# Gate biases beside their products, and earlier operand loads for the recurrence, in a two-layer diffusion step

## The chip, the cores and the metric

The kernel runs on 1 core of a Trainium2 chip. The metric is the device time of one execution in microseconds (us), lower is better. Times of a kernel are given as the median of several runs; a profile comes from one more execution, whose own time is given beside its span.

## The reference, cut to what matters

One inference step of a two-layer hybrid backbone (model width 1024) on 256 context tokens and 1024 latent tokens. Layer 0 combines grouped-query attention (8 query heads, 2 key heads of 64) with a bidirectional RWKV-7 recurrence (8 heads of 64); layer 1 is gated linear attention (GLA). Each layer is modulated: a vector m of 3072 numbers gives shift, scale and gate.

```
m = silu(cond) @ mod_w[i] + mod_b[i]
shift, scale, gate = split(m, 3)
h = rms_norm(x, norm_g[i]) * (1 + scale) + shift
out = mixer_i(h)                  # i = 0: attention + RWKV-7, i = 1: GLA
x = x + gate * out

# attention: 128-query blocks, keys and values of the cache (512) and the latent tokens (1024)
p = softmax(q @ k.T * 64 ** -0.5);  o_a = (p @ v) * silu(ga)

# RWKV-7, per head, forward and backward over the tokens
sa = s @ (-kk_t)
s  = s * w_t + outer(sa, kk_t * a_t) + outer(v_t, k_t)
y_t = s @ r_t
```

## The kernel before, in words

The program is recorded by a scheduler of its own (`Sched`), which holds a planned start for each engine, queue and tile. The kernel's parts are written as *streams* of *tasks* (generators). `drive` looks at the next dozen instructions of each running task, plans when each could start, and records the one with the lowest planned start; where two engines could do an operation it picks one. So the instruction order on every engine comes out of planned costs, and one edit can move a great many rows. All instructions are recorded through one line (L357), which is why all rows carry that line; the tile names tell what they are. `get(tag)` takes a tile of a tag's set of buffers, `put` gives it back, `sch.until(cond)` holds a task until a flag is set.

Phases in the order of time: norms and modulation; the projections of layer 0, the last of which are those of the gates (`gated`, tiles `gt`, two buffers); then the *mixers* of layer 0, about 510 to 1340 us; output projection; layer 1. This case turns on the passage from the gate projections into the mixers. There these streams run beside each other:

- `room_attn` and `room_rwkv` make room: they close the pools of the phase that ends, open new ones, and write the constants of the new phase. `room_attn` allocates KA, KB (keys of the two key heads; KA the high, KB the low part and a row of ones), VO (values) and the query tiles QA, QB, and fills the unused rows of KB on POOL (GpSimd), 4 memsets. `room_rwkv` waits until the eight gate projections are over (it takes over their SBUF), then loads the masks (gmask, zmask, m1) and makes id16, m116, hm, id2, the fills of UV, LL and Z, and the ring of states, and at its end sets flag `rwkv`.
- `rwkv_seg`: 40 tasks (4 head pairs x 5 segments of 256 tokens x 2 directions), 4 at a time. Each loads AR, BK and Vs (3 buffers each), scales with `pair` by the decays, multiplies AR by BK on PE (TensorE), inverts a triangular matrix in five rounds (tiles TT, Tm, LT, Z), builds GR, UV, U, GH, and carries the state along (tile `ring`).
- `maxima` (one task per unit of 512 or 256 queries): scores KA x QA, a maximum over each row on DVE (VectorE; `mx`), and at the end of 12 such products one transpose (`ident,mx`) whose result goes into QB as the row's offset.
- `attend`: for each block of 128 keys the pair QA x KA + QB x KB, exp on ACT (ScalarE), and the product with VO. It waits for flag `keys`.
- `keys` loads KB and VO once `attn` is set.
- `mods`: 16 chunks of 256 columns of the modulation, for layer 0's gate and for layer 1. Of each, `mod_cols` loads 1 MB of weights (`mw`, 1 buffer) and multiplies them by sT (16 matmuls); the 8 gate chunks also load a bias row. Products lie in tile m4 (1 buffer), and the bias in a `gt` tile.

The bias tile is the one that the gate projections use, two buffers in all:

```
b = yield from get(row, False)        # row = "gt"
D.dma_start(out=b[0:2, 0:n], in_=I["mod_b"][...].to_broadcast([2, n]))
```

All loads named here go through SP's queue, in SP's order; each load waits there until an earlier one of at most 8 has landed.

## Time and profile before

| | |
|---|---|
| median of 3 runs | 2095.14 us (2094.4 to 2097.18) |
| the profiled execution | 2095.28 us, its span 2093.5 us |
| busy share of the span: PE, DVE, ACT, POOL | 95%, 69%, 48%, 14% |
| mean granted clock of PE | 0.984 of full |
| share of the chain that ended last: PE, DVE, issue, ACT, DMA | 52%, 11%, 4%, 3%, 1% |
| PE busy from 560 to 1240 us | 664.32 of 680 us |
| PE busy from 510 to 540 us | 5.31, 6.37 and 7.61 in stretches of 10 us |

How to read it: the median of runs and the profiled execution differ by 0.14 us, so sums below are made against 2095.28. PE is busy nearly all the time, but not evenly; the profile cuts the span in 40 slices, and the digit of PE is below 9 in four of them: the first, the tenth (about 471 to 523 us, with the passage into the mixers), the 26th (about 1309 to 1361 us, the output projection) and the last. A slice is 52 us, so gaps of a few us are seen only in the timeline.

### The profile page before, as it was taken

What the parts mean: (1) busy time and instruction counts of PE and PEld (TensorE: products, weight loads), DVE (VectorE), ACT (ScalarE), POOL (GpSimd) and SP (SyncE); (2) the same over time, 40 slices, a digit from 0 to 9 for tenths busy, and PEclk for the clock granted to TensorE, in tenths of its full rate; (3) what the DMA queues carried; (4) which work ended last, traced back from release to release, by engine and by line L of the source; (5) the groups of instructions that cost most, each with busy time, mean ns of one, the idle gap of its engine ahead of it and who ended that gap; (6) DMA issues with size and microseconds to landing.
All of it is one profiled execution on the core that took longest, in us unless ns stands there. A gap on an engine that the chain in (4) does not pass through costs nothing.

```text
span 2093.5 us, 38539 instructions
## 1 busy us (share of the span) xinstructions
PE 1997.0 (95%) x14876; PEld 1557.7 (74%) x14876; DVE 1452.4 (69%) x2879; ACT 1007.6 (48%) x2184; POOL 289.9 (14%) x383
## 2 busy tenths in 40 slices
PE   6999999998999999999999999799999999999998
PEld 4878687886667777777776766578778888888886
DVE  4677866777887888778888987453575656564455
ACT  4454744553556655665656563333445454542111
POOL 2010200013221112121110020010121111110011
PEclk9999999999999999999999999899999999999999
DMA  8224342527513241323223224342102011115653
GB/s 297 71 101 159 138 164 81 179 91 238 170 54 103 81 143 59 97 74 111 78 68 88 67 70 143 95 146 73 50 14 64 28 50 29 49 31 165 192 170 112
DMA packets 215143, 219.56 MB, mean 105 GB/s; under 512 B 16480, under 2 KB 161232, under 8 KB 214960
## 3 DMA queue, kind: packets, MB, share of 16 engines
q1 hardware_dynamic: 214960, 217.10, 33.0%
q8 instruction: 117, 1.92, 0.4%
q14 instruction: 66, 0.54, 0.1%
HBM read 149.63 MB, written 67.39 MB: 104 GB/s over the span
## 4 chain that ended last, share of the span: by engine, by line
PE 52%; DVE 11%; issue 4%; ACT 3%; DMA 1%; POOL 0%; SPq 0%; POOLq 0%; DVEq 0%; ACTq 0%
PE a L357 26%; PE pj L357 26%; DVE QQ L357 2%; DVE LL L357 1%; DVE mx L357 1%; ACT QQ L357 1%; DVE TT L357 1%; DVE dec L357 1%; DVE gt L357 1%; DVE Z L357 1%; DVE y L357 1%; DVE GR L357 0%; DVE KX L357 0%; DVE GH L357 0%; DVE Ad L357 0%
## 5 line engine op out<-in xcount | busy, mean ns | idle before, releaser
L357 PE MATMUL pj<-hhi,whi 128*128 128x512 f32 (+1 forms) x672 | 241.1, 361 | 2.6 <-DVE whi L357 1.4
L357 PE MATMUL pj<-hhi,wlo 128*128 128x512 f32 (+1 forms) x672 | 240.4, 360 | 1.6 <-DVE wlo L357 1.6
L357 PE MATMUL pj<-hlo,whi 128*128 128x512 f32 (+1 forms) x672 | 241.3, 361 | 0.6 <-DVE hlo L357 0.6
L357 PEld LDWEIGHTS pj<-hhi,whi 128*128 128x128 f32 x672 | 128.9, 192 | 26.4 <-issue 3.7
L357 PEld LDWEIGHTS pj<-hhi,wlo 128*128 128x128 f32 x672 | 128.9, 192 | 24.0 <-issue 4.1
L357 PEld LDWEIGHTS pj<-hlo,whi 128*128 128x128 f32 x672 | 129.1, 192 | 23.7 <-issue 5.8
L357 POOL TENSOR_TENSOR acc<-acc,pt 128x512 f32<-128x512 f32 (+1 forms) x57 | 73.0, 1286 | 389.3 <-ACT pt L357 190.5
L357 PE MATMUL a<-h1hi,whi 128*128 128x512 f32 (+2 forms) x304 | 111.9, 369 | 0.0
L357 PE MATMUL a<-h1lo,whi 128*128 128x512 f32 (+2 forms) x304 | 111.0, 366 | 0.0
L357 PE MATMUL a<-h1hi,wlo 128*128 128x512 f32 (+1 forms) x296 | 109.9, 371 | 0.0
L357 PE MATMUL pj<-h1hi,whi 128*128 128x512 f32 (+2 forms) x296 | 108.4, 366 | 1.5 <-ACT h1hi L357 0.8
L357 PE MATMUL pj<-h1lo,whi 128*128 128x512 f32 (+2 forms) x296 | 108.4, 366 | 0.0
L357 PE MATMUL pj<-h1hi,wlo 128*128 128x512 f32 (+1 forms) x280 | 102.4, 366 | 0.0
L357 DVE TENSOR_TENSOR acc<-acc,pt 128x512 f32<-128x512 f32 (+1 forms) x127 | 90.6, 736 | 14.4 <-ACT pt L357 9.5
L357 PE MATMUL a<-pt,VO 128*64 128x512 f32 (+1 forms) x368 | 95.9, 605 | 0.0
L357 POOL TENSOR_SCALAR sq<-sq 128x1 f32<-128x1 f32 x70 | 19.9, 284 | 510.2 <-ACT gt L357 225.1
L357 DVE TENSOR_REDUCE mx<-pj 128x1 f32<-128x512 f32 (+1 forms) x118 | 75.4, 653 | 3.3 <-PE pj L357 3.1
L357 DVE TENSOR_REDUCE mx<-a 128x1 f32<-128x512 f32 x90 | 59.1, 669 | 10.8 <-PE a L357 10.7
L357 ACT ACTIVATE pt<-pj 128x512 f32<-128x512 f32 (+1 forms) x105 | 60.8, 597 | 10.2 <-PE pj L357 7.8
L357 PE MATMUL pj<-woh,oh 128*128 128x512 f32 (+1 forms) x160 | 61.5, 384 | 3.9 <-DVE oh L357 3.9
L357 PEld LDWEIGHTS a<-h1hi,whi 128*128 128x128 f32 (+1 forms) x304 | 56.9, 187 | 9.5 <-DVE gt L357 0.8
L357 PEld LDWEIGHTS pj<-h1hi,whi 128*128 128x128 f32 (+1 forms) x296 | 55.5, 188 | 11.2 <-ACT h1hi L357 1.2
(509 smaller groups left out, 5477.0 us busy)
## 6 DMA issues: line engine op xcount, KB each, us to landing
mw<-in_mod_w SPq DMA_DIRECT2D x24, 1024.0 KB
ws<-wk SPq DMA_DIRECT2D x32, 512.0 KB
wst<-in_ev_w_in SPq DMA_DIRECT2D x26, 512.0 KB
wst<-in_od_w_in SPq DMA_DIRECT2D x24, 512.0 KB
AR<-ws SPq DMA_DIRECT2D x40, 256.0 KB
BK<-ws SPq DMA_DIRECT2D x40, 256.0 KB
wst<-o SPq DMA_DIRECT2D x14, 512.0 KB
Vs<-vt SPq DMA_DIRECT2D x80, 64.0 KB
```

What stands on the lines that cost most here:

```text
L357: r = f(*a, **k)
```

## The change

1. `mod_cols` takes no bias tile any more. For the gate chunks it takes m4 when the load of the weights is issued, and loads the bias into columns n to 2n of that tile, beside the products. So m4 is held from the load on, and `gt` belongs to the gate projections alone.
2. `room_attn` no longer fills KB on POOL; `load_keys(v, 1)` fills KB of one key head on DVE, two memsets, just before the load of that KB.
3. `keys` waits for the flag `segs` beside `attn`.
4. `room_rwkv` allocates y, AR, BK and Vs directly after the loads of the masks, and there sets `segs`.
5. `rwkv_seg` waits for `segs` ahead of its loads and for `rwkv` ahead of its first `pair`.

```
-    def mod_cols(i, c0, n, bank, row, ready=lambda: True):
+    def mod_cols(i, c0, n, bank, ready=lambda: True):
...
             if a == 0 and c0 >= 2 * DM:
-                b = yield from get(row, False)
-                D.dma_start(out=b[0:2, 0:n], in_=I["mod_b"][i:i + 1, c0:c0 + n].to_broadcast([2, n]))
+                m4 = yield from get("m4", False)
+                b = m4[0:2, n:2 * n]
+                D.dma_start(out=b, in_=I["mod_b"][i:i + 1, c0:c0 + n].to_broadcast([2, n]))
...
-        m4 = yield from get("m4", False)
+        if c0 < 2 * DM:
+            m4 = yield from get("m4", False)
...
-            V.tensor_tensor(b[0:2, 0:n], p[0:2, :], b[0:2, 0:n], ALU.add)
-            V.tensor_scalar(m[0:2, :], b[0:2, 0:n], 0.5, 0.0, ALU.mult, ALU.add)
-            put(row, b)
+            V.tensor_tensor(b, p[0:2, :], b, ALU.add)
+            V.tensor_scalar(m[0:2, :], b, 0.5, 0.0, ALU.mult, ALU.add)
...
         load_keys(0, 0)
-        for v in range(2):
-            G.memset(KB[v][64:128, :].bitcast(F32), 0.0)
-            G.memset(KB[v][64:65, :].bitcast(F32), 1.0)
...
         else:
+            V.memset(KB[v][64:128, :].bitcast(F32), 0.0)
+            V.memset(KB[v][64:65, :].bitcast(F32), 1.0)
             D.dma_start(out=KB[v][0:64, :].bitcast(F32), in_=src)
 
     def keys():
 
-        yield from sch.until(lambda: flags["attn"])
+        yield from sch.until(lambda: flags["attn"] and flags["segs"])
...
+        slots("y", 2, [P, T], pool=rn)
+        slots("AR", 3, [P, 3, 4, 64])
+        slots("BK", 3, [P, 2, 4, 64])
+        slots("Vs", 3, [P, 2, 2, 64])
+
+        def loads():
+            flags["segs"] = True
+        sch.then(loads)
         id16 = rc.tile([P, P], F16, name="id16")
...
-        slots("y", 2, [P, T], pool=rn)
-        slots("AR", 3, [P, 3, 4, 64])
-        slots("BK", 3, [P, 2, 4, 64])
-        slots("Vs", 3, [P, 2, 2, 64])
...
     def rwkv_seg(p, d, seg, st, step):
         t0 = seg * SEG
-        yield from sch.until(lambda: flags["rwkv"])
+        yield from sch.until(lambda: flags["segs"])
...
+        yield from sch.until(lambda: flags["rwkv"])
         pair(AR[:, 2], id2.unsqueeze(1).to_broadcast([P, 4, 64]), last.to_broadcast([P, 4, 64]), ALU.mult)
```

How the change moves instructions, at the passage into the mixers. First SP's queue, from the load of the first query tiles on; before, with the masks and the loads of the first segments (AR, BK, Vs) behind keys, values and the second query tiles:

```order
L357 DMA QB_3838<-qh_101 64x512
L357 DMA KB_3827<-kh 64x1792
L357 DMA VO<-vo 128x1792
L357 DMA gb_100<-gt_132 128x512
L357 DMA mw_3831<-in_mod_w 128x8x256
L357 DMA QA_3835<-qh_101 64x512 x2
L357 DMA QB_3839<-qh_101 64x512
L357 DMA gmask<-in_k_gmask 128x256
L357 DMA zmask<-in_k_zmask 128x640
```

and with the change:

```order
L357 DMA QB_3838<-qh_101 64x512
L357 DMA mw_3831<-in_mod_w 128x8x256
L357 DMA m_0_3832<-in_mod_b 2x256
L357 DMA gb_100<-gt_132 128x512
L357 DMA gmask<-in_k_gmask 128x256
L357 DMA zmask<-in_k_zmask 128x640
L357 DMA gsq_3908<-in_k_m 128x256
L357 DMA AR_3911<-ws_75 128x512
L357 DMA BK_3914<-ws_75 128x512
```

The masks and the first segments' loads have moved ahead of VO, KB and the second query tiles, which now follow the third segment's Vs.

Second, DVE behind the sum of a gate projection (`gt_132<-gt_132,pj_142`). Before, the first 12 row maxima and their last reduction come first, and the constants of the recurrence follow; from the last of the 12 on:

```order
L357 TENSOR_REDUCE mx_3842<-pj_142 128x1
L357 TENSOR_REDUCE mx_3842<-mx_3842 128x4
L357 SCALAR_TENSOR_TENSOR gt_132<-gt_132,pj_140 128x512
L357 CAST id_3944<-ident 128x128
L357 MEMSET hm 128x2
L357 MEMSET hm 64x1 x2
L357 TENSOR_TENSOR id_3947<-ident 128x64
```

and with the change:

```order
L357 SCALAR_TENSOR_TENSOR gt_133<-gt_133,pj_140 128x512
L357 CAST id_3920<-ident 128x128
L357 MEMSET hm 128x2
L357 MEMSET hm 64x1 x2
L357 TENSOR_TENSOR id_3923<-ident 128x64
L357 COPY Z_0_3945<-id_3920 128x64x4
L357 COPY Z_0_3947<-id_3920 128x16x16
L357 TENSOR_SCALAR LL_0_3949<-ident 128x4x128
L357 MEMSET KB_3827 64x1792
L357 MEMSET KB_3827 1x1792
L357 TENSOR_REDUCE mx_3842<-a_147 128x1
```

The constants and the two memsets of KB now stand ahead of the 12 maxima. The second set of 12 (`mx_3843`), which before ends two rows ahead of the first scaling of AR, now comes during and after the first segments.

Third, PE behind the first products of the recurrence (`AR,BK`, then the transposes `ident,BT`). Before, the first pair of attention stands between the first segment's products and the second's:

```order
L357 MATMUL pj_140<-ident,BT_3959 128x128 x4
L357 MATMUL a_147<-QA_3834,KA_3825 128x512
L357 MATMUL a_147<-QB_3838,KB_3827 128x512
L357 MATMUL pj_143<-AR_3951,BK_3954 128x128
L357 MATMUL a_144<-AR_3951,BK_3954 128x128
```

and with the change, from the last of the first 12 scores to the first segment's products, and from their end on:

```order
L357 MATMUL a_146<-KA_3825,QA_3834 128x512
L357 MATMUL pj_142<-mw_3831,sT_3833 32x256 x8
L357 MATMUL pj_142<-m_0_3832,msel 2x256
L357 MATMUL pj_140<-ident,mx_3842 4x128
L357 MATMUL a_147<-AR_3911,BK_3914 128x128
```

```order
L357 MATMUL pj_143<-AR_3911,BK_3914 128x128
L357 MATMUL pj_141<-ident,BT_3924 128x128 x4
L357 MATMUL a_144<-AR_3912,BK_3915 128x128
L357 MATMUL a_146<-AR_3912,BK_3915 128x128
L357 MATMUL a_144<-AR_3912,BK_3915 128x128
```

With the change the first segment follows the first transpose of maxima (before: the second), and no pair of attention stands on PE before the first product with `ring`; before, 11 pairs did, and 4 groups of products with VO or with the sums. Counted on PE from the first score to the first product with `ring`, the change has 9 score products, 11 pairs, 8 products with VO and one chunk of the modulation (8 mw,sT rows) fewer and 4 rows U,LL more; all of these come later. The PE order is the same in both up to the first scores and from shortly after the mixers' end; the first product with `ring` stands 40 rows earlier than before.

## Rows read from the trace of the kernel before

**Rows 1.** The page: span, and PE in it.
```profile
span 2093.5 us, 38539 instructions
```

**Rows 2.** Windows: stretch, us, busy per engine (instructions), clock, DMA share, GB/s.
```profile
560.00:1240.00 680.00, 664.32 (x7147) 496.55 (x7147) 569.37 (x1264) 406.82 (x1004) 103.61 (x103) 1.00 0.27 82
```

**Rows 3.** Timeline of PE: start, us, operation, count, idle before and releaser.
```profile
509.26 0.39 PE L357 MATMUL pj<-hhi,wlo 128*128 128x512 f32 x1
514.69 0.77 PE L357 MATMUL a<-KA,QA 128*128 128x512 f32 x1 [5.04 <-DMA QA<-qh]
...
523.01 0.27 PE L357 MATMUL a<-ident,mx 128*4 128x128 f32 x1 [2.98 <-DVE mx L357]
...
532.61 1.20 PE L357 MATMUL pj<-mw,sT 128*32 128x256 f32 x16 [1.83 <-DVE mx L357]
534.26 0.37 PE L357 MATMUL a<-ident,mx 128*4 128x128 f32 x1 [0.45 <-DVE mx L357]
534.56 0.58 PE L357 MATMUL a<-AR,BK 64*128 64x128 f32 x1
```

**Rows 4.** Timeline of DVE, the two sets of maxima.
```profile
515.49 0.69 DVE L357 TENSOR_REDUCE mx<-a 128x1 f32<-128x512 f32 x1 [7.84 <-PE a L357]
...
522.79 0.17 DVE L357 TENSOR_REDUCE mx<-mx 128x4 f32<-128x12 f32 x1
...
534.06 0.14 DVE L357 TENSOR_REDUCE mx<-mx 128x4 f32<-128x12 f32 x1
```

**Rows 5.** Timeline of POOL, fills of KB and LL.
```profile
502.07 6.43 POOL L357 MEMSET KB<- 64x1792 f32 x4
...
515.67 1.83 POOL L357 MEMSET LL<- 128x1024 f32 x2
```

**Rows 6.** DVE's groups by form: busy, mean ns | idle before.
```profile
L357 DVE MEMSET on<- 96x1024 f32 x1 | 0.9, 912 | 0.3 <-DVE h1lo L357 0.3
```

**Rows 7.** Timeline of SP's queue, first masks and operands.
```profile
517.42 0.53 SPq L357 DMA_DIRECT2D gmask<-in_k_gmask  x1
...
527.74 0.57 SPq L357 DMA_DIRECT2D AR<-ws  x1
```

**Rows 8.** Timeline of DVE, first rounds of the inversion.
```profile
543.34 0.43 DVE L357 CAST_PREDICATED Z<-zmask,pj 128x256 f16<-128x256 int32 x1
...
545.24 0.45 DVE L357 CAST_PREDICATED Z<-zmask,a 128x256 f16<-128x256 int32 x1 [0.55 <-PE a L357]
...
554.51 0.40 DVE L357 TENSOR_TENSOR TR<-TT,a 128x256 fp32r<-128x256 f16 x1
```

**Rows 9.** Timeline of PE, fillers and the first ring product.
```profile
549.82 1.08 PE L357 MATMUL a<-pt,VO 128*64 128x512 f32 x4
...
553.18 0.40 PE L357 MATMUL pj<-QA,KA 128*128 128x512 f32 x1
553.41 0.40 PE L357 MATMUL pj<-QB,KB 128*128 128x512 f32 x1
...
558.29 1.14 PE L357 MATMUL pj<-U,LL 128*128 128x128 f32 x8
...
566.54 0.34 PE L357 MATMUL pj<-ring,GH 128*64 128x64 f32 x4
```

**Rows 10.** Windows of 2.5 us at the recurrence's start, columns as above.
```profile
537.50:540.00 2.50, 2.50 (x17) 1.85 (x18) 2.44 (x6) 1.38 (x4) 1.26 (x2) 0.50 0.37 88
540.00:542.50 2.50, 1.57 (x19) 1.08 (x17) 2.25 (x6) 1.27 (x4) 0.00 (x0) 0.95 0.72 195
```

**Rows 11.** Windows of 10 us at the recurrence's start.
```profile
550.00:560.00 10.00, 9.71 (x92) 6.43 (x92) 9.83 (x21) 4.55 (x10) 4.37 (x6) 1.00 0.33 78
```

**Rows 12.** PE's waits from 1240 to 1350 us: engine, tile, releaser, total, times, longest.
```profile
PE a L357 <- DMA QB<-mr: 3.0, 1, 3.0
PE pj L357 <- DVE mx L357: 2.0, 1, 2.0
...
PE pj L357 <- ACT gsq L357: 0.6, 1, 0.6
```

More of the change, by code (lines that the diff above doesn't have):

```diff
@@ L717, in tile_hybrid_dit_step @@
     left, segs, right = (ctx.enter_context(ExitStack()) for i in range(3))
-    flags = dict(left=0, gates=0, attn=False, keys=0, rwkv=False, mods=False, normed=False, gla=False, gl=False, units=0, weights=0, lr=0, begun=0, ra=False)
+    flags = dict(left=0, gates=0, attn=False, keys=0, rwkv=False, mods=False, normed=False, gla=False, gl=False, segs=False, units=0, weights=0, lr=0, begun=0, ra=False)
     def pool(stack, name, **k):
@@ L896, in mods @@
             yield from sch.until(lambda: loads[0] >= (5 if n % 2 else 1))
-            yield from mod_cols(0, n * 512, 512, "a", "xr", lambda: modded[0] and modded[1])
+            yield from mod_cols(0, n * 512, 512, "a", lambda: modded[0] and modded[1])
             def done():
@@ L1303, in mods @@
             for c in range(c0, 3 * DM, 256):
-                yield from mod_cols(i, c, 256, "b", "gt")
+                yield from mod_cols(i, c, 256, "b")
         def done():
```

## The prediction, written before the changed kernel was run

> **What bounds the kernel now.** I read the page first, then the timeline at the place of the change, then the waits behind it. PE is busy for nearly all of the recurrence: 664.32 of the 680 us from 560 to 1240, with DVE at 569.37 behind it [rows 1, 2]. So over that stretch an instruction that PE executes costs its time wherever it stands, and a shift of the order alone changes nothing; what can change the end are the gaps of PE ahead of this stretch and behind it, and stretches at half clock. The gaps ahead lie at the passage. The last gate projection starts at 509.26 and lasts 0.39; the first score starts at 514.69, held 5.04 by the query load; the first transpose of maxima waits 2.98 for DVE, the modulation's products 1.83 and the second transpose 0.45; then, at 534.56, the first AR,BK of the recurrence [rows 3]. It stands directly behind the second transpose, so it is the second set of maxima that lets the recurrence start, although its operands (AR issued at 527.74 [rows 7]) come late too. The first product with the ring starts at 566.54 [rows 9]. I take this product as the mark at which the dense stretch begins.
>
> **The change, part by part.** *First scores.* The loads of KA and the first QA keep their place in SP's queue and PE its order up to the scores, so the 5.04 us stay: 0.
>
> *Start of the recurrence.* Only one set of maxima stands ahead of AR,BK now, but on DVE the constants and the two memsets of KB stand ahead of that set. The DVE write of LL waits for POOL's fill: the two fills start at 515.67 and take 1.83, so the first is over at about 516.6 [rows 5]; with half a us for the write, DVE is free at 517.1. The memsets: 1792 elements each; the one comparable DVE row takes 912 ns for 1024 [rows 6], so 912 x 1792 / 1024 = 1.60, two of them 3.2 us. POOL needs 6.43 for four of the same shape, 1.61 each [rows 5], the same price, so I take 3.2. DVE reaches the first maximum at 520.3 instead of 515.49. The set takes 522.79 - 515.49 = 7.3 us as before [rows 4], to 527.6; the bias sum, m116 and the last reduction take some 1.0, and the transpose to the first AR,BK 0.3 (534.26 to 534.56 [rows 3]): 528.9. Before it was 534.56, so **5.7 us earlier**. The masks, issued at 517.42, and AR at 527.74 [rows 7] move ahead of VO, KB and the second query tiles in SP's queue, so I expect the operands by then; if they land later this shrinks. Bounds: 2.5 earlier if the memsets cost double, 8.9 if they cost nothing.
>
> [...]
>
> *The chain to the ring.* Before it takes 566.54 - 534.56 = 32.0 us [rows 3, 9]. No pair of attention stands in it any more. One round of the inversion, with little waiting, takes 545.24 - 543.34 = 1.90 [rows 8]; five take 9.5, where before it is 554.51 - 543.34 = 11.2: 1.7 saved. Between 554.51 and the ring, PE also executed 3 pairs, 4 scores and a VO group: a pair costs twice 553.41 - 553.18 = 0.23, a score 0.23, a VO group 1.08 [rows 9], together 3.4. PE and DVE are both full there (9.71 and 9.83 of 10 [rows 11]), but the chain also waits on its own steps; I take half, 1.7. So the ring starts **3.4 us earlier by this, 9.1 with the earlier start**. Bounds: 0, if the chain's own steps set it, and 8.4, if PE's work does (9.4 of fillers less 1.0 for the second segment's U,LL, 1.14 per 8 [rows 9]).
>
> *The work that is put off.* Up to the ring PE now executes 11 pairs, 9 scores, 4 VO groups and one modulation chunk less. At the prices above 11 x 0.46 = 5.1, 9 x 0.23 = 2.1, 4 x 1.08 = 4.3 [rows 9]; the chunk 1.20 [rows 3] and 0.3 for its small products = 1.5. Together 13.0, less 1.1 for a U,LL that comes ahead: **11.9 us** that come later. Since PE idles only 15.7 us in the 680 that follow, they cannot hide there but lengthen it, or come behind the last segment. Bounds: half of it, 6, if it lands in those gaps, to 11.9. I take 11.9.
>
> *The tail.* The recurrence ends earlier, and attention that is left over lies in the stretch behind it, where PE waited 3.0 for a QB load, 2.0 for maxima and 0.6 for gsq [rows 12]: 5.6 us which more work can fill, though DVE is busy there too. I take half, **2.8**, bounds 0 and 5.6.
>
> *The rest.* The gate projection's ACT operation no longer waits for a `gt` buffer; PE has no row that waits for it: 0. KB of the second key head is filled on DVE amid the recurrence, 3.2 us in a DVE that idles 111 of 680 [rows 2]; hidden, at worst 3.2. A bias in m4 means that a gate chunk's weights cannot be joined by their bias before the chunk ahead has given m4 back; the chunks are needed only at the layers' ends: 0.
>
> Sum, against the profiled execution's 2095.28 (0.14 above the median of the runs): 2095.28 - 9.1 + 11.9 - 2.8 = **2095.3 us**. Differences under 0.2%, 4.2 us, can hardly be told from none, so I call it no change: an earlier start paid back by later attention.
>
> **The rivals.** *A, as above.* Own range 2090.5 to 2100, from the chain's and the tail's bounds taken half way.
>
> *B, faster: the fillers cost the chain their full price.* PE and DVE were both above 9.7 of 10 in the stretch [rows 11], which speaks for it; that the round of 1.90 contains waits of DVE for PE [rows 8] speaks against. Then the ring starts 5.7 + 8.4 = 14.1 earlier: 2095.28 - 14.1 + 11.9 - 2.8 = 2090.3; if half of the work put off also lands in the 15.7 us of gaps, 2084.3. Middle 2087.
>
> *C, slower: the start of the recurrence runs at half clock without its fillers.* [...] A stretch of 2.5 us at 0.50 loses 1.25; two of them and 3.6 of waits that the fillers had covered cut the 9.1 to 3: 2095.28 - 3 + 11.9 - 2.8 = 2101.4, and 2104.2 if the tail fills nothing. It decides from where the ring starts less than 5 us earlier. [...] Against it: the clock was 1.00 from 550 to 560 [rows 11], and two segments start at once now.
>
> *D, the change doesn't do what it says.* The first AR,BK comes no earlier, as the masks or operands land late or DVE's constants wait longer for POOL. Then only the chain's 3.4 remain: 2095.28 - 3.4 + 11.9 - 2.8 = 2101.0.
>
> **How the numbers follow.** A 0.45, B 0.29, C 0.18, D 0.08. A puts 0.04 below 2091 and 0.03 above 2099.3, B is nearly all below, C and D nearly all above. Faster 0.32, same 0.42, slower 0.26. The range reaches to the middle of B and into C: 2085 to 2103.
>
> **What would show it.** In the changed profile: first maximum at about 520.3 behind two KB memsets of 1.6 each; first AR,BK near 529; first ring product near 557.5; no pair before it; the granted clock from 530 to 555 at 1.00 for the most part (else C); the last product with the ring some 9 us earlier than now, the last attention product at about the same time as now. Wrong if the ring starts before 553 (B) or after 561 (C, D), or if the stretch from the ring to the last attention product doesn't grow by some 9 us.

## The result, and the profile after

The changed kernel takes 2105.86 us in the median of 6 runs (2101.52 to 2108.96), the kernel before 2094.6 us (2092.5 to 2097.18): a ratio of 1.0051, 95% interval 1.0038 to 1.0064. It is slower by 0.5%. The profiled execution of the changed kernel took 2101.52 us, the fastest of its six; a second profile of the same kernel (`after_again`, below), with a span of 2105.7 us, lies nearer to the median, so both stand beside each other where it matters.

The page of the changed kernel, its span and PE's busy time:

```profile
span 2099.7 us, 38560 instructions
...
PE 1996.4 (95%) x14876; PEld 1556.0 (74%) x14876; DVE 1461.5 (70%) x2860; ACT 1009.9 (48%) x2193; POOL 297.8 (14%) x393
```

Its timeline of PE at the marks of [rows 3, 9]: the last gate projection, first score, transpose of the maxima, first AR,BK, first and last product with the ring, and last product with VO:

```profile
510.39 0.39 PE L357 MATMUL pj<-hhi,wlo 128*128 128x512 f32 x1
515.33 0.77 PE L357 MATMUL a<-KA,QA 128*128 128x512 f32 x1 [4.55 <-DMA QA<-qh]
...
533.58 0.27 PE L357 MATMUL pj<-ident,mx 128*4 128x128 f32 x1 [1.17 <-DVE mx L357]
533.78 0.37 PE L357 MATMUL a<-AR,BK 64*128 64x128 f32 x1
...
563.14 0.34 PE L357 MATMUL pj<-ring,GH 128*64 128x64 f32 x4
...
1223.52 0.34 PE L357 MATMUL pj<-ring,GH 128*64 128x64 f32 x4
...
1331.57 0.60 PE L357 MATMUL a<-pt,VO 128*64 128x256 f32 x4
```

In the kernel before, the last two marks stand at 1240.23 and 1322.33. So the recurrence ends 17 us earlier, and the attention behind it ends 9 us later. At the front the first AR,BK comes only 0.8 us earlier (534.56 to 533.78) and the ring 3.4.

Why the front gains so little is seen on DVE. Its timeline in the changed kernel, from the cast of the identity (`id16`) to the first maximum:

```profile
512.05 0.78 DVE L357 CAST id<-ident 128x128 f16<-128x128 f32 x1
512.77 0.30 DVE L357 MEMSET hm<- 128x2 f32 x3
513.08 0.23 DVE L357 TENSOR_TENSOR id<-ident 128x64 f32<-128x64 f32 x1
515.58 5.64 DVE L357 COPY Z<-id 128x256 f16<-128x256 f16 x2 [2.27 <-POOL Z L357]
521.14 0.41 DVE L357 TENSOR_SCALAR LL<-ident 128x512 f32<-128x512 f32 x1
521.96 1.55 DVE L357 MEMSET KB<- 64x1792 f32 x1 [0.41 <-issue]
523.94 1.55 DVE L357 MEMSET KB<- 1x1792 f32 x1 [0.43 <-DVE KB L357]
525.52 0.69 DVE L357 TENSOR_REDUCE mx<-a 128x1 f32<-128x512 f32 x1
```

and POOL's timeline over the same time:

```profile
510.90 1.85 POOL L357 MEMSET UV<- 128x1024 f32 x2 [7.61 <-PE pj L357]
512.69 1.92 POOL L357 MEMSET LL<- 128x1024 f32 x2
514.56 2.38 POOL L357 MEMSET Z<- 128x512 f16 x5
516.89 1.84 POOL L357 MEMSET LL<- 128x1024 f32 x2
518.68 2.39 POOL L357 MEMSET Z<- 128x512 f16 x5
```

Two small copies into Z take 5.64 us, and end at 521.22, when POOL's unbroken row of fills ends (518.68 + 2.39 = 521.07). The groups by form show two very different times for the same copy (busy in us, mean ns of one; the two slow copies overlap, so both means count the hold). First the kernel before:

```profile
L357 DVE COPY Z<-id 128x256 f16<-128x256 f16 x4 | 0.8, 234 | 0.0
```

and of the changed one:

```profile
L357 DVE COPY Z<-id 128x256 f16<-128x256 f16 x2 | 5.6, 5138 | 2.3 <-POOL Z L357 2.3
```

The clock after the first AR,BK: windows of 2.5 us of the changed kernel (columns as in [rows 10]):

```profile
537.50:540.00 2.50, 0.68 (x8) 0.47 (x9) 2.43 (x7) 2.09 (x5) 0.00 (x0) 1.00 0.64 186
540.00:542.50 2.50, 1.20 (x16) 0.94 (x16) 2.47 (x6) 1.50 (x4) 0.33 (x1) 0.81 0.23 80
542.50:545.00 2.50, 2.13 (x33) 1.88 (x33) 1.44 (x4) 1.24 (x3) 0.71 (x1) 0.50 0.00 0
...
552.50:555.00 2.50, 2.50 (x19) 2.31 (x18) 1.55 (x4) 0.96 (x2) 0.00 (x0) 0.50 0.52 150
555.00:557.50 2.50, 2.50 (x27) 2.49 (x25) 2.08 (x5) 0.69 (x2) 0.00 (x0) 0.96 0.39 109
```

From 542.5 to 555 PE runs at 0.50 of the full clock, behind two windows in which it was busy for 0.68 and 1.20 us of 2.50. In the kernel before it ran at 0.50 from 535 to 540, in the window of [rows 10] and the one ahead of it:

```profile
535.00:537.50 2.50, 2.50 (x21) 2.28 (x20) 1.15 (x3) 0.81 (x2) 1.39 (x2) 0.50 1.07 317
```

The stretch that answers to [rows 2], and the one behind the last ring product, once with all work and once (the last row) with the products with VO alone; the changed kernel:

```profile
560.00:1240.00 680.00, 665.36 (x7145) 496.54 (x7144) 573.97 (x1255) 409.23 (x1014) 115.92 (x116) 1.00 0.29 88
...
1224.60:1332.40 107.80, 99.36 (x452) 58.09 (x452) 74.62 (x113) 44.86 (x81) 18.60 (x12) 0.98 0.37 119
...
1224.60:1332.40 107.80, 25.79 (x104) 6.82 (x104) 0.98 0.37 119
```

and the kernel before, over its own stretch of the same meaning:

```profile
1242.00:1323.10 81.10, 74.06 (x353) 47.63 (x352) 55.55 (x85) 33.26 (x60) 7.09 (x8) 0.96 0.44 133
...
1242.00:1323.10 81.10, 19.22 (x76) 5.17 (x76) 0.96 0.44 133
```

PE is as full in the recurrence as it was. Behind it, 104 products with VO are left instead of 76, and PE idles 8.4 us instead of 7.0: the extra work did not go into the gaps. The waits of PE there (total, times, longest), to be compared with [rows 12]:

```profile
PE a L357 <- DVE mx L357: 5.2, 4, 2.6
```

The wait for the QB load (3.0) is gone, and waits for maxima have taken its place.

### The profile page after: what moved, and what is told of

It is laid out like the page before. It is cut to its first block, busy times and chain, and to the rows that moved or that the text cites. A ratio compares the mean times of both kernels' runs of the same rounds, so it can differ in the third digit from the quotient of the medians.

```text
span 2099.7 us, 38560 instructions
## 1 busy us (share of the span) xinstructions
PE 1996.4 (95%) x14876; PEld 1556.0 (74%) x14876; DVE 1461.5 (70%) x2860; ACT 1009.9 (48%) x2193; POOL 297.8 (14%) x393
## 5 line engine op out<-in xcount | busy, mean ns | idle before, releaser
L357 PE MATMUL pj<-hhi,whi 128*128 128x512 f32 (+1 forms) x672 | 241.2, 362 | 2.9 <-DVE whi L357 1.4
L357 PE MATMUL pj<-hlo,whi 128*128 128x512 f32 (+1 forms) x672 | 241.6, 361 | 1.1 <-DVE hlo L357 1.1
L357 PE MATMUL pj<-hhi,wlo 128*128 128x512 f32 (+1 forms) x672 | 240.6, 360 | 1.6 <-DVE wlo L357 1.6
L357 PEld LDWEIGHTS pj<-hhi,whi 128*128 128x128 f32 x672 | 129.1, 192 | 26.4 <-issue 3.7
L357 PEld LDWEIGHTS pj<-hlo,whi 128*128 128x128 f32 x672 | 129.2, 192 | 25.0 <-issue 6.2
L357 PEld LDWEIGHTS pj<-hhi,wlo 128*128 128x128 f32 x672 | 129.2, 192 | 24.0 <-issue 4.1
L357 POOL TENSOR_TENSOR acc<-acc,pt 128x512 f32<-128x512 f32 (+1 forms) x55 | 72.6, 1326 | 375.3 <-ACT pt L357 207.2
L357 PE MATMUL a<-h1hi,whi 128*128 128x512 f32 (+2 forms) x304 | 112.5, 370 | 0.7 <-ACT whi L357 0.7
L357 PE MATMUL a<-h1lo,whi 128*128 128x512 f32 (+2 forms) x304 | 112.2, 369 | 0.0
L357 PE MATMUL a<-h1hi,wlo 128*128 128x512 f32 (+1 forms) x296 | 109.8, 371 | 0.1
L357 DVE TENSOR_TENSOR acc<-acc,pt 128x512 f32<-128x512 f32 (+1 forms) x129 | 95.8, 765 | 18.5 <-ACT pt L357 17.8
L357 PE MATMUL pj<-h1hi,whi 128*128 128x512 f32 (+3 forms) x296 | 107.2, 363 | 0.8 <-ACT h1hi L357 0.8
L357 PE MATMUL pj<-h1lo,whi 128*128 128x512 f32 (+3 forms) x296 | 106.5, 361 | 0.0
L357 PE MATMUL pj<-h1hi,wlo 128*128 128x512 f32 (+1 forms) x280 | 101.8, 364 | 0.0
L357 PE MATMUL a<-pt,VO 128*64 128x512 f32 (+1 forms) x368 | 95.6, 602 | 0.0
L357 POOL TENSOR_SCALAR sq<-sq 128x1 f32<-128x1 f32 x70 | 20.1, 287 | 506.1 <-ACT gt L357 221.9
L357 DVE TENSOR_REDUCE mx<-pj 128x1 f32<-128x512 f32 (+1 forms) x118 | 76.2, 661 | 2.5 <-PE pj L357 2.2
L357 PE MATMUL pj<-woh,oh 128*128 128x512 f32 (+1 forms) x184 | 68.9, 375 | 4.0 <-DVE oh L357 4.0
L357 PE MATMUL pj<-woh,ol 128*128 128x512 f32 (+1 forms) x184 | 68.9, 375 | 0.8 <-DVE ol L357 0.8
L357 PE MATMUL pj<-wol,oh 128*128 128x512 f32 (+1 forms) x184 | 68.6, 373 | 0.0
L357 ACT ACTIVATE pt<-pj 128x512 f32<-128x512 f32 (+1 forms) x97 | 56.3, 592 | 20.1 <-PE pj L357 18.6
L357 PEld LDWEIGHTS a<-h1hi,whi 128*128 128x128 f32 (+1 forms) x304 | 57.0, 188 | 10.4 <-ACT whi L357 0.9
```

Of the source, the lines that this page charges most:

```text
L357: r = f(*a, **k)
```

## The experiments

*Theory 1, the hold:* copies, casts and multiplications by a scalar (`tensor_scalar`) of DVE stand still in this passage while POOL fills without a break; the change brings such operations, and everything behind them on DVE, under POOL's fills. 1b: if the copies are taken away, the next such operation is held instead. *Theory 2, the order behind:* part of the change makes the planner leave more attention behind the recurrence. *Rivals:* the fills of KB on DVE are the loss by the time that they take; or the half clock in the chain to the ring is the loss. An expectation that numbers a further theory says what it is.

To compare executions, times are counted from E, the end of the last gate projection (the start of the first score less its wait: 515.33 - 4.55 = 510.8 in the changed kernel); E itself lies between 507.9 and 511.6 from profile to profile. The table gives, in us, the first maximum (mx), first AR,BK and first ring product after E, the times from first to last ring product and from there to the end of the last VO product (tail), all of one profile each; then the median of the runs less that of the kernel before on the same chip, and the ratio's 95% interval, which is some 2 us to either side. The last ring product is here the last row that reads the ring (`GH,ring`), 1 to 2 us behind the mark used above.

| kernel | mx | AR,BK | ring | to last ring | tail | median less before | ratio |
|---|---|---|---|---|---|---|---|
| before | 5.8 | 24.9 | 56.8 | 675.6 | 81.1 | | |
| after | 14.7 | 23.0 | 52.3 | 661.6 | 107.7 | +11.3 | 1.0038 to 1.0064 |
| after_again | 14.7 | 23.0 | 52.7 | 663.1 | 109.1 | +11.9 | 1.0046 to 1.0072 |
| z_act | 14.5 | 22.8 | 52.5 | 662.9 | 109.2 | +11.4 | 1.0044 to 1.0069 |
| z_ll_act | 7.4 | 15.6 | 45.3 | 661.3 | 109.4 | +4.9 | 1.0016 to 1.0037 |
| z_ll_act_kb_pool | 6.6 | 14.9 | 45.5 | 661.7 | 108.0 | +3.4 | 1.0012 to 1.0029 |
| z_ll_act_dup | 6.5 | 15.1 | 44.1 | 661.3 | 109.5 | +4.5 | 1.0017 to 1.0035 |
| bias_only | 12.0 | 29.1 | 59.4 | 660.1 | 119.2 | +26.9 | 1.0121 to 1.0150 |
| bias_zll | 5.6 | 22.7 | 52.4 | 660.8 | 117.7 | +20.4 | 1.0086 to 1.0114 |
| segs_only | 5.3 | 21.4 | 52.6 | 660.8 | 107.4 | +6.9 | 1.0024 to 1.0048 |
| kbdve_only | 5.4 | 29.5 | 60.9 | 658.7 | 94.0 | +1.3 | 0.9997 to 1.0017 |
| bias_segs_keys | 12.0 | 20.5 | 51.3 | 661.2 | 101.3 | +0.1 | 0.9993 to 1.0019 |
| bs_zll | 5.8 | 16.7 | 46.8 | 669.9 | 100.0 | +2.8 | 1.0001 to 1.0018 |
| bsk_zll | 5.7 | 14.2 | 44.8 | 661.2 | 101.2 | -5.7 | 0.9964 to 0.9983 |
| kb0_dve_zll | 14.8 | 23.1 | 53.9 | 661.2 | 101.3 | +3.6 | 1.0009 to 1.0030 |
| kb1_dve_zll | 10.7 | 19.2 | 49.5 | 661.9 | 108.2 | +7.8 | 1.0022 to 1.0047 |
| bsk_all | 5.9 | 14.1 | 44.2 | 661.1 | 101.8 | -4.2 | 0.9969 to 0.9989 |
| kb0_dve_all | 6.7 | 16.5 | 45.7 | 662.7 | 102.1 | -3.4 | 0.9968 to 0.9990 |
| kb1_dve_all | 6.4 | 14.6 | 44.2 | 661.7 | 109.4 | +4.9 | 1.0016 to 1.0035 |

**The hold.** The changed kernel as it is, then with the two copies into Z executed by ACT, with the write of LL as well, and with the fills of KB on POOL too. Each is changed at the line that issues an instruction (L357), behind the planner, so that the order of all other rows stays (the three edits are written here as one):

```
-        r = f(*a, **k)
+        copy = name == "dve" and f.__name__ == "tensor_copy" and writes[0][0] == "Z"                # z_act
+        mul = name == "dve" and f.__name__ == "tensor_scalar" and writes[0][:2] == "LL"            # z_ll_act
+        fill = name == "dve" and f.__name__ == "memset" and writes[0][:2] == "KB"                  # z_ll_act_kb_pool
+        r = (self.nc.scalar.copy(*a) if copy else self.nc.scalar.mul(*a[:3]) if mul
+             else self.nc.gpsimd.memset(*a) if fill else f(*a, **k))
```

> The changed kernel itself once more, for a second profile and as the base of the other three. Theory 1 (a stalled start and half clock, then attention work put off): 2102 to 2108 us again. If the spread of its six earlier runs (2101.5 to 2109.0, mean granted clock 0.983 to 0.980) is a matter of how long PE stays at half clock behind the passage, this profile shows a longer stretch at 0.50 between 540 and 570 us where its time is longer than 2101.5. A rival, that the spread comes from transfers, expects the same stretch at 0.50 and longer waits for DMA.

> Of the changed kernel only the two f16 copies into Z that DVE executes at the passage are executed by ACT. In the changed kernel these two take 5.64 us together (515.58 to 521.22), where six such took 0.22 each before, while POOL fills LL and Z until 521.07. Theory 1a (only the f16 copies are held by POOL): DVE writes LL at 518, the first maximum comes at 522, the first AR,BK at 530.3, 3.5 us earlier, and the time falls by 3 us. Theory 1b (the write of LL is held by POOL too): DVE's write of LL ends at 521.5 as now, and nothing changes. Rival (POOL has nothing to do with it, the copies wait for something else such as id16): the copies take long on ACT as well.

> As before this one, and the one write of LL that DVE executes there goes to ACT too, so that DVE goes from the small constants (done at 513.3) straight to the two fills of KB. Theory 1: these run from 513.5 to 517, the first maximum comes at 517, the first AR,BK at 525.5 to 526.5 (8 us earlier than in the changed kernel), the first ring product at 555 to 557, and the time falls by 5 to 8 us to about 2098. Rival 1c (fills by DVE are held by POOL as well): the two fills end at 521 or later, the first AR,BK at 530. Rival 2 (half clock sets the chain, not its start): the chain to the ring grows by as much as its start comes earlier, and the time stays at 2105.

> As the one before, and the fills of KB go back to POOL, where they come behind the fills of LL and Z. Theory 1: DVE is free for the maxima at 516 as in the kernel before, the first AR,BK comes at 524 to 525, 1 to 1.6 us earlier than with the fills on DVE, unless its operands land later than that; the time falls by another 1 us. Rival: the operands (AR issued at 515.2) land at 526 or so and set the start, and nothing more is gained.

The second profile of the changed kernel, though 6 us longer, has no longer stretch at 0.50 between 540 and 570 (542.5 to 552.5, then 0.59), so the half clock there does not explain how far the runs lie apart; what does stays open.

`z_act` changes nothing in the time. ACT executes the copies amid the same fills of POOL, five of them in 2.20 us, so it is not their data that held them. The timeline of DVE shows why the time stays: the operation behind the copies is held in their place (0.42 us in the kernel before, 0.41 in the changed one).

```profile
514.78 2.20 ACT L357 COPY Z<-id 128x256 f16<-128x256 f16 x5
...
517.47 3.48 DVE L357 TENSOR_SCALAR LL<-ident 128x512 f32<-128x512 f32 x1 [4.56 <-POOL LL L357]
```

With that one on ACT too, in `z_ll_act`, DVE is free at once, beside the same fills of POOL (511.46 to 519.83 there):

```profile
512.51 1.55 DVE L357 MEMSET KB<- 64x1792 f32 x1 [0.43 <-issue]
514.49 1.55 DVE L357 MEMSET KB<- 1x1792 f32 x1 [0.43 <-DVE KB L357]
516.91 0.69 DVE L357 TENSOR_REDUCE mx<-a 128x1 f32<-128x512 f32 x1 [0.86 <-PE a L357]
```

The memsets are not held and cost 1.55 each, the maximum waits for PE alone, the ring comes 7.4 us sooner after E, and the time falls by 7.0 us (from +11.9 to +4.9). So 1 and 1b hold. Moving the KB fills to POOL gives 1.5 us (+4.9 to +3.4, with intervals that overlap): by their own time they are a small part of the loss. 3.4 us stay.

**The half clock.** `z_ll_act` with 120 products of the inversion executed twice up to the first ring product:

```
+        if name == "pe" and writes and not hasattr(self, "ringed"):
+            if any(x.startswith("ring") for x in reads):
+                self.ringed = True
+            elif any(x.startswith(("TT", "LT")) for x in reads) and k.get("start", True) and k.get("stop", True):
+                self.tc.keep_in_program_order(f(*a, **k))
```

> The version with Z and LL on ACT, in which each of the 120 small products of the inversion's rounds that stand ahead of the first ring product is executed twice (the second overwrites the first with the same numbers), so that PE is busier between the rounds; 120 x 0.03 us is 3.6 us of additional work at the full clock. Theory 3 (half clock sets a part of the chain): the granted clock between 535 and 547 rises from 0.50, the ring product comes 1 to 3 us earlier than 554.9, and the time falls by as much. Rival (the chain is set by the hops between the engines, and the clock costs nothing there): the ring product comes 2 to 4 us later by the additional work, and so does the end. If the clock stays at 0.50 in spite of the duplicates, the run tells the two apart only in that the duplicates then cost up to 7 us.

The windows from 520 to 550, first of `z_ll_act` and then of this kernel:

```profile
520.00:550.00 30.00, 24.11 (x228) 19.32 (x226) 24.22 (x56) 12.01 (x29) 8.14 (x21) 0.72 0.67 187
```

```profile
520.00:550.00 30.00, 24.07 (x345) 20.58 (x346) 25.36 (x57) 12.40 (x27) 6.25 (x18) 0.89 0.67 186
```

117 more products fit into the same busy time of PE at a clock of 0.89 instead of 0.72. The ring comes 1.2 us sooner after E, but the time stays (+4.5 beside +4.9). The half clock is real, but it is not the loss: what lifting most of it gives at the ring can't be told from none in the time.

**Each part alone.** The bias beside the products (part 1); early operands (parts 4 and 5); KB on DVE (part 2); all but part 2:

```
 # bias_only, in mod_cols (the other rows as in the change)
-                b = yield from get(row, False)
+                m4 = yield from get("m4", False)
+                b = m4[0:2, n:2 * n]
 # segs_only, in room_rwkv (y, AR, BK, Vs and this flag ahead of id16) and in rwkv_seg
+            flags["segs"] = True
...
-        yield from sch.until(lambda: flags["rwkv"])
+        yield from sch.until(lambda: flags["segs"])
...
+        yield from sch.until(lambda: flags["rwkv"])
 # kbdve_only, in load_keys, for both heads; gone from room_attn, where it was on G
+            V.memset(KB[v][64:128, :].bitcast(F32), 0.0)
+            V.memset(KB[v][64:65, :].bitcast(F32), 1.0)
 # bias_segs_keys: the whole change without the rows of kbdve_only
```

> The kernel before with part 1 of the change alone (the bias beside the products; KB filled by POOL and the loads of the recurrence as before). Its order puts DVE's constants, among them all six f16 copies into Z and the writes of LL, ahead of the first maxima, while POOL fills KB, UV, LL and Z to about 520. Theory 1 (DVE is held by POOL's fills): these constants end only when POOL's fills do, the first maximum comes at 521 to 523 instead of 515.5, the first AR,BK at 535 or later, and the time is 4 to 10 us above before. Rival (the hold belongs to the changed order of loads, not to POOL): the constants take 3 us, the first maximum comes at 516 to 517, and the time is within 2 us of before.

> The kernel before with parts 4 and 5 alone (tiles of AR, BK and Vs first, their loads before the constants). Its order keeps the first twelve maxima ahead of DVE's constants, so that these come after 522, when POOL's fills are over; AR,BK stands ahead of the second transpose, and 7 pairs, 7 scores and 4 VO groups come after the first ring product that stood ahead of it. Theory 1: no DVE row is held (copies of Z 0.2 to 0.3 each), the first AR,BK at 530 to 531, the ring product at 560 to 562, the work put off is about 8 us and the time is 2096 to 2099. Rival 2 (an earlier start is a net gain as long as DVE is not held): 2090 to 2093.

> The kernel before with part 2 alone. The two fills of KB stand on DVE directly behind the fill of ones, so they run while PE waits 5 us for the query load, and DVE's f16 copies come after the first maxima, when POOL has finished. Theory 1: the first maximum comes when the first score is done, or 0 to 1.5 us later, no copy is held, the first AR,BK comes a little later than before as the first pair of attention and a third modulation chunk stand ahead of it, and the time is 2095 to 2099. Rival (fills of KB on DVE cost their 3.2 us wherever they stand): the first maximum 3 us later and 2098 or more.

> The changed kernel without part 2: KB is filled by POOL ahead of UV, LL and Z, as in the kernel before. DVE's constants, all of them, stand ahead of the first maxima. Theory 1: POOL's fills run to 521, and so do DVE's copies; the first maximum comes at 522 to 524, the first AR,BK at 530 to 532, 2 us earlier than in the changed kernel, as the two fills of KB (3.1 us and two gaps of 0.4) have left DVE; the time is 2102 to 2106. Rival (the fills of KB on DVE are what costs): the first maximum at 517, the time below 2098.

The parts don't add up. The bias alone costs 26.9 us, far more than expected, with a tail of 119.2 us, 38 longer than before, behind a recurrence that is only 15.5 shorter. Early operands cost 6.9 with a start that is not held (first maximum 5.3 after E), more than theory 1 expected, and where rival 2 saw a gain. KB on DVE alone costs nothing that can be told, its fills running while PE waits for the queries:

```profile
507.99 1.55 DVE L357 MEMSET KB<- 64x1792 f32 x1 [0.41 <-issue]
509.98 1.55 DVE L357 MEMSET KB<- 1x1792 f32 x1 [0.43 <-DVE KB L357]
511.56 0.69 DVE L357 SCALAR_TENSOR_TENSOR gt<-gt,pj 128x512 f32<-128x512 f32 x1
```

And `bias_segs_keys`, expected slower, equals the kernel before although its copies are held 5.64 us like the change's: its tail is 101.3 where the change has 107.7 to 109.1. So part 2, in company with the others, costs behind the recurrence.

**Parts without the hold.** ACT executes the copies into Z and the ring and the write of LL (`copy` now by what is read):

```
+        copy = name == "dve" and f.__name__ == "tensor_copy" and reads[0][:3] in ("id1", "id2")
 # bias_zll: on bias_only; bsk_zll: on bias_segs_keys; bs_zll: bsk_zll, with keys as before:
-        yield from sch.until(lambda: flags["attn"] and flags["segs"])
+        yield from sch.until(lambda: flags["attn"])
```

> The version with part 1 alone (2122.5 us), with DVE's copies into Z and ring and its write of LL at the passage on ACT; PE's order is the same. Theory 1: the first maximum comes 5 to 6 us sooner, and the time falls by 4 to 6 us to about 2117; what remains above before is work of PE and waits in a worse order, which this doesn't touch. Rival (the hold is what all 27 us follow from): below 2105.

> The changed kernel without part 2 (KB filled by POOL ahead of the other fills), and all of DVE's copies into Z and ring and its write of LL at the passage executed by ACT; the order of PE is that of the version without part 2. Theory 1 (DVE's copies are held by POOL, and this start is what can be gained): the first maximum 4 to 5 us sooner after the last gate projection than without it (12.0 there, 6 to 7.5 here), the first AR,BK 4 to 5 us sooner, and the time falls to 2091 to 2093, below the kernel before. Rival (the copies on ACT come so late that the recurrence waits for them, or the gain is lost at half clock): the ring product comes less than 2 us sooner and the time stays at 2095.

> As the one before, with part 3 left out too: KB and VO load ahead of the recurrence's operands, so parts 1, 4 and 5 remain. Theory 1: DVE is free at the first score as there; five score products stand among the first rounds. If the order of KB and VO matters little, as no pair of attention comes before the ring product in either, the time is that of the one before within 2 us; the rival, that the later operands hold the start, has the first AR,BK 2 to 4 us later and the time 2 to 4 us higher.

The hold is worth 6.5 us in `bias_zll` and 5.8 in `bsk_zll`, which at 2090.24 us (2095.97 before) is faster than both kernels. Without part 3 (`bs_zll`) it is 8.5 us worse, where at most 4 were expected: the first AR,BK comes 2.5 us later, as the rival said, but the larger loss is a recurrence of 669.9 us instead of 661.2.

**Which key head's fill.** `bsk_zll`, with KB of one head filled on DVE by `load_keys`, that of the other by POOL ahead, first with the cast of `id16` on DVE and then (`_all`) on ACT:

```
-        for v in range(2):
-            G.memset(KB[v][64:128, :].bitcast(F32), 0.0)
-            G.memset(KB[v][64:65, :].bitcast(F32), 1.0)
+        G.memset(KB[1][64:128, :].bitcast(F32), 0.0)      # kb0; for kb1: KB[0]
+        G.memset(KB[1][64:65, :].bitcast(F32), 1.0)
...
+            if v == 0:                                     # kb0; for kb1: v == 1
+                V.memset(KB[v][64:128, :].bitcast(F32), 0.0)
+                V.memset(KB[v][64:65, :].bitcast(F32), 1.0)
...
+        copy = name == "dve" and f.__name__ == "tensor_copy" and (writes[0][:4] == "id16" or reads[0][:3] in ("id1", "id2"))    # _all
```

> The changed kernel with Z, ring and LL on ACT at the passage, the KB of the first key head filled on DVE as in the change, that of the second filled by POOL ahead of the phase as before. If the second head's fills amid the recurrence are what makes the order worse: first maximum 1 to 2 us later than with both on POOL, the stretch from the last ring product to the last attention product near 101 us, 2090 to 2093 us. If the first head's fills are: that stretch near 109 and 2098 to 2101 us.

> The same with the fills the other way round: the first key head's KB by POOL ahead of the phase, the second's by DVE amid the recurrence. If the second head's fills make the order worse: the stretch behind the last ring product near 109 us, 2097 to 2100 us. If the first head's do: near 101 us and 2090 to 2092 us. If both orders are near 101, or both near 109, the planner's order depends on more than where the fills stand, and no single fill is the cause.

> bsk_zll with the cast into id16 on ACT as well; no row of PE moves. In bsk_zll that cast took 1.67 us on DVE, so theory 1 (DVE operations held by POOL's fills) expects the first maximum up to 1.5 us sooner after the last gate projection and about 2089 to 2090 us; the rival (what is held is only passed on to the next wait, the first query load or the operands) expects the time of bsk_zll, 2090.2.

> kb0_dve_zll (first key head's KB filled on DVE, the second's on POOL ahead) with the cast into id16 on ACT as well, where it took 9.02 us on DVE behind POOL's fills. Theory 1 expects no hold on DVE any more: first maximum some 9 us sooner after the last gate projection (about 6), the first product with the ring near 45 after it instead of 53.9, about 101 us from the last ring product to the last attention product, and so 2090 to 2092 us. The rival (the fill of the first head's KB on DVE costs what the hold cost) expects 2098.

> The reverse: first key head's KB on POOL ahead, second's on DVE amid the recurrence; the cast into id16 on ACT. Theory 2 (the second head's fill amid the recurrence leaves more attention behind the last ring product) expects about 108 us from the last ring product to the last attention product as in kb1_dve_zll, no hold at the start, and 2096 to 2099 us, 6 to 8 slower than bsk_all. The rival (that tail came of the late start) expects about 101 us there and 2090 us.

In the first two the tails came as expected (101.3 and 108.2), but a hold came back at the cast of `id16`, a tile that POOL's fills don't write. POOL and DVE in `kb0_dve_zll`:

```profile
508.23 1.85 POOL L357 MEMSET UV<- 128x1024 f32 x2 [3.46 <-PE pj L357]
...
515.93 2.38 POOL L357 MEMSET Z<- 128x512 f16 x5
```

```profile
509.38 9.02 DVE L357 CAST id<-ident 128x128 f16<-128x128 f32 x1
```

The cast ends at 518.40, the fills at 518.31. It started 1.15 us behind POOL's first fill, just as in the changed kernel (512.05 and 510.90), where it passed in 0.78; what made the difference is not known. On ACT it is held no more: `kb0_dve_all` goes from +3.6 to -3.4, 7.1 us down, with the first maximum 8.1 sooner after E. `bsk_all` gains nothing over `bsk_zll`, as its rival said. And the two heads part clearly: the first head's fill on DVE costs 0.7 us (-4.2 to -3.4, within the intervals), the second's 9.1 (-4.2 to +4.9), with the start no later and the tail at 109.4 instead of 101.8. That fill stands amid the recurrence; DVE in `kb1_dve_all`:

```profile
767.81 1.55 DVE L357 MEMSET KB<- 64x1792 f32 x1 [0.43 <-issue]
...
793.82 1.55 DVE L357 MEMSET KB<- 1x1792 f32 x1 [0.43 <-issue]
```

The windows there, first of `bsk_all`, then of `kb1_dve_all`, which are within 0.3 us of each other in PE over the three windows of 66 us ahead of this one:

```profile
752.00:818.00 66.00, 64.33 (x746) 51.55 (x744) 59.80 (x135) 39.45 (x106) 9.07 (x11) 1.00 0.34 102
```

```profile
752.00:818.00 66.00, 62.48 (x713) 49.12 (x713) 62.13 (x131) 39.08 (x106) 10.71 (x13) 1.00 0.28 86
```

PE loses 1.85 us of busy time and 33 products in this window, at the place where DVE is busiest. The time on DVE is not the reason, though: `z_ll_act_kb_pool` has the order of the change with both fills executed by POOL at their places (757.43 and 790.56), where DVE is no busier than in `bsk_all`; PE loses 1.24 us and 23 products all the same, and the tail is 108.0:

```profile
752.00:818.00 66.00, 63.09 (x723) 50.43 (x721) 59.72 (x132) 39.09 (x107) 12.37 (x13) 1.00 0.32 98
```

A second loss, of 1.27 us, stands where no fill of KB is, again first in `bsk_all` and then in `kb1_dve_all` (63.87 us of PE in `z_ll_act_kb_pool`):

```profile
950.00:1016.00 66.00, 65.06 (x721) 50.05 (x721) 59.15 (x133) 41.47 (x105) 8.50 (x8) 1.00 0.31 93
```

```profile
950.00:1016.00 66.00, 63.79 (x719) 48.70 (x718) 58.48 (x132) 37.02 (x98) 6.08 (x7) 1.00 0.29 87
```

At the end 452 products of PE stand in the tail where `bsk_all` has 445, 104 of them with VO instead of 94, and PE's busy time there is 101.84 instead of 95.24:

```profile
1215.50:1317.30 101.80, 95.24 (x445) 56.78 (x443) 72.81 (x112) 40.73 (x75) 13.62 (x10) 0.97 0.38 117
```

```profile
1215.40:1324.80 109.40, 101.84 (x452) 59.73 (x450) 74.57 (x112) 45.36 (x82) 18.26 (x12) 0.95 0.37 117
```

## Why the prediction was wrong

The loss of 11.9 us (`after_again`) can be followed through the runs. The other parts without the hold gain 4.2 us (`bsk_all`). With both KB fills in the change's order, still without the hold, the time is +4.9 (`z_ll_act`), 9.1 more; the second head's fill alone gives the same +4.9 (`kb1_dve_all`), and the first head's alone 0.7, which can't be told from none. With the hold it is +11.9, 7.0 more (6.5 by `z_act`). The steps of 9.1 and 7.0 us are medians against the kernel before on two chips, each good to some 2 to 4 us.

- **Start of the recurrence: failed.** "DVE is free at 517.1" was to put the first maximum at 520.3 and AR,BK at 528.9. It priced the wait of the LL write for its fill, and put the copies into Z, which stand ahead of it, at nothing. They were held until POOL was through, so DVE was free at 521.5 and the first maximum came at 525.52; AR,BK came 0.8 us earlier instead of 5.7, and the ring at 563.14, behind the 561 that was named for rivals C and D. The fills of KB, sized at 1.60 each, took 1.55. Rival D had the outcome ("DVE's constants wait longer for POOL") at a chance of 0.08, which was too low for a wait whose two sides were both in sight: DVE's constants moved ahead of the maxima, and POOL's fills beside them. Its sum of 2101.0 still lies 4.9 us short of the 2105.86 measured; that part is not the start's. Without the hold the start gains 9.3 us after E (`z_ll_act`, 24.9 to 15.6), more than the forecast, since KB's fills then run while PE waits for the query load.

The kernel's own planner shows how the order came about. It has a term for such a wait (`_beside`, which adds the time that DVE waits for POOL or POOL for DVE), but POOL's memsets are left out of it (`late = op != "memset"`), so it placed the copies under the fills as if they were free there.

Beside POOL's fills the runs show three kinds of DVE operation standing still: COPY (5.64 us for two in the changed kernel, a mean of 0.23 for one in the kernel before), TENSOR_SCALAR (3.48 in `z_act`, 0.42 before) and CAST (9.02 in `kb0_dve_zll`, 0.22 before). Three others took their own time beside them: the reduction (0.69) and the memset (1.55) in `z_ll_act`, and the TENSOR_TENSOR (0.23) in the changed kernel. The hold outlasted single fills: the cast of `kb0_dve_zll`, which started at 509.38, stood from within the second (two took 1.85 from 508.23) to the end of the last of POOL's 16 fills (518.31). The runs show the hold; its cause was not shown.

- **The chain to the ring: right in size.** 32.0 us before, 29.4 after, where 32.0 - 3.4 = 28.6 was expected. The half clock of rival C lies in it, 0.50 from 542.5 to 555; it did not decide, as `z_ll_act_dup` lifts most of it and keeps its time. Rival C's sum took two stretches of 2.5 us at 0.50, with 1.25 us lost in each, and 3.6 of waits; no run shows these losses by themselves. What the runs showed is 0.50 in five stretches of 2.5 us in the changed kernel (542.5 to 555), and, at a mean clock of 0.89 instead of 0.72 from 520 to 550, a ring 1.2 us sooner after E (`z_ll_act_dup` against `z_ll_act`). Whether the chain got shorter for the reasons given (quicker rounds, half of the fillers) was not tested.
- **The work put off: near in size, in part by luck.** From the first ring product to the last VO product it is 769.3 us (after_again 772.2) against 756.7: 12.6 to 15.5 more, where 11.9 was expected before the tail's share. But `bsk_all`, which executes about as much up to the ring (281 products of PE, 282 in the changed kernel), needs 762.9, only 6.2 more. The rest came with the order around the second head's fill, which the prediction had at nothing.
- **The tail fills 2.8: failed.** PE's idle time behind the last ring product went from 7.0 to 8.4 us. A wait for a load was freed, and waits for maxima came instead.
- **"Hidden, at worst 3.2" for the second head's KB fill: failed.** It was costed as time on a DVE that idles 111 of 680 us. The runs show 9.1 us, and not by that time, since the loss of PE stays when POOL executes the fills: it comes with the order that the planner makes around them.
- **The bias: 0 was no sound price by itself.** Alone it costs 26.9 us; what it costs in company no run shows, as none takes it alone out of the change. Why the order without the other parts is so much worse is not settled; what is shown is that the most of it lies behind the first ring product (779.3 us to the last VO product, 756.7 before).
- The end was expected at no change since an earlier start was to pay for the attention put off. The start was not earlier, and the attention had to be paid.

What stays open: why the planned order with the second fill leaves 10 more VO products behind the recurrence. PE loses 1.85 us in the fill's window and 1.27 in the one from 950 to 1016; which waits of that order do it was not followed. Whether the order alone does it, or a fill at that place on any engine, was not told apart: `z_ll_act_kb_pool` still fills there, on POOL.

## What to carry to other kernels

Before operations of DVE are moved, lay POOL's timeline beside their new place: a copy or cast of 0.2 us under an unbroken row of fills took up to 9 us here, and all of DVE behind it waited; giving three small operations to ACT turned +11.9 us into +4.9. If one held operation is taken away, look at the next of its kind, which inherited the wait here (the write of LL, 3.48 us in `z_act`). Where a planner decides the order, look at what its costs leave out, here POOL's memsets. And price a small operation in a full stretch by the order that comes out of it, not by its own time: two memsets of 1.55 us, moved, cost 9 us, and parts that lose alone (26.9 and 6.9 us) gained 4 to 6 together with part 3 once the hold was gone.

## What was not expected of the hardware

A DVE operation was held through a whole row of POOL's instructions, not only one: the cast of `id16` in `kb0_dve_zll` took 9.02 us and ended 0.09 us after the last fill, where in the changed kernel the same cast took 0.78 and ended at 512.83, as POOL went over from the fills of UV (to 512.75) to those of LL (from 512.69). In `bias_segs_keys` it took 1.67. In all three it started 1.15 us behind the first fill (509.14 and 507.99 in `bias_segs_keys`); what lets it pass was not tried. The clock stayed at 0.50 from 542.5 to 555 in the changed kernel although PE was busy for 2.50 of 2.50 us from 550 on.
